# In the routing phase GpSimd, not VectorE, writes the low part of the weight tiles

## The chip, the core and the metric

One core of one Trainium2 chip runs the whole program in one launch. The metric is the device time of that core in microseconds (us); lower is better. TensorE (PE in the profile) multiplies matrices, VectorE (DVE) and ScalarE (ACT) work element by element, GpSimd (POOL) is the fourth compute engine, and SyncE (SP) issues most of the DMAs here.

## What is computed

Two decoder layers over 512 tokens of width 1024, in float32. Each layer has a mixer (a gated MLP and a stick-breaking attention side by side) and then a PEER layer: product keys choose 16 of 16384 single-neuron experts for each of 8 heads of each token. Cut to the PEER layer:

```
q1, q2 = split(h @ w_q)                 # 8 heads, 128 = 64 + 64
s1, s2 = q1 @ k1.T, q2 @ k2.T           # 128 keys each
v1, i1 = top_k(s1, 16); v2, i2 = top_k(s2, 16)
sc, pos = top_k(v1[:, None] + v2[None, :], 16)   # of 256 sums
eidx = i1 * 128 + i2, taken at pos
g = softmax(sc)
y = sum_k g_k * gelu(u_tab[eidx_k] . h) * v_tab[eidx_k]
```

## The kernel before

**How the PEER layer is done.** For 384 of the 512 tokens the kernel gathers no rows: it multiplies all 16384 rows of `u_tab` with the tokens (128 tiles of 128 experts, "ut tiles"), applies GELU, scales by a dense matrix of gates that is zero where an expert was not chosen, and multiplies with all of `v_tab`. The other 128 tokens go by indirect DMAs that GpSimd issues. A layer therefore has three phases: `mixer`, `route_phase` and `dense_phase`.

**Weights in two parts.** TensorE multiplies in a reduced float32 format (`F32R`), so each weight tile of 128x1024 is split into a high part and the rest, and a product takes three matmuls (`mm3`, L308 to L313: hi*hi, lo*hi, hi*lo). The class `Stream` (L51) does this for every weight: `_load` (L61) issues the DMA of a raw tile on SP's queue, `_prep` (L76) lets ScalarE write the high part (`whi`, L83) and VectorE subtract it from the raw tile to get the low part (`wlo`, L84). The pool `wp` has three buffers of each part; `fill` (L92) keeps two tiles prepared ahead of the one that TensorE uses. ScalarE can write a new `whi` once TensorE has done with the tile three places earlier.

**The routing phase** (L623, twice, once for each layer) first computes the queries of the 8 heads (`pq`, 8 weight tiles), their scores against the keys (`sc`), and on VectorE the top 16 of each row of 128 scores (L676 to L680: MAX8, FIND_INDEX8 and MATCH_REPLACE8). Then comes `route` (L715) for each of four blocks of 128 tokens: the top 16 of the candidate sums, and the expert indices by comparisons and sums over `f16` tiles of 128x2048 (L746 to L766). `build` (L793) makes the gate matrix for three blocks: for 24 pieces VectorE writes two one-hot tiles (L806, L807) and scales one by the gates (L809, L810), each 128x2048 `f16`; TensorE multiplies them (`pg`, L816, L817), ScalarE copies the product into `sg` (L818) and a DMA writes it to DRAM. Nothing of this uses GpSimd, but for 32 memsets of constants (L705, L706) after the top 16 of the scores, since their buffers take the place of those that it used.

**What fills TensorE meanwhile.** `prefill` (L635) computes the first 60 ut tiles of the layer (`PRE`, L29) during the routing: 24 matmuls `pA` of 384 columns each, GELU on ScalarE (`ga`, L645), and a DMA to DRAM, from where the dense phase loads them again. `prefill` and the generator `routing` are interleaved by estimated costs (L830 to L841).

**Order.** The program is written in one stream and a scheduler sorts each engine's instructions with a simulated timeline; the instructions of `_prep` get a higher priority (L81). The order on each engine is fixed when the program is built. An engine takes its instructions in that order and waits where one is not ready.

**Dense phase.** The remaining ut tiles and all v tiles go through the same `_prep`; the gates are loaded by `load_g` (L853).

Of the kernel before, what the change touches and what calls it, by code (L numbers as in the profile page):

```python
# [9 lines left out]
F32 = mybir.dt.float32  # L10
# [40 lines left out]
class Stream:  # L51


    def __init__(self, tc, raw, part, entries, dma_ahead, prep_ahead, start=None):
        self.tc, self.nc = tc, tc.nc
        self.raw, self.part = deque(raw), part
        self.src, self.loaded, self.ready, self.plain = deque(entries), deque(), deque(), deque()
        self.da, self.pa = dma_ahead, prep_ahead
        self.start, self.held, self.preps = start, RAW1 if start else 0, 3 if start else 0

    def _load(self):  # L61
        kind, ap = self.src.popleft()
        r = self.raw[0].tile([P, 1024], F32, tag="raw", name="raw")
        self.raw.rotate(-1)
        r = r[:, : ap.shape[-1]]
        if self.held:
            self.held -= 1
            self.start("dma", self.nc.gpsimd.dma_start(r, ap))
        else:
            self.nc.sync.dma_start(r, ap)  # L70
        if kind == "a":
            self.plain.append(r)
        else:
            self.loaded.append((kind, r))

    def _prep(self):  # L76
        kind, r = self.loaded.popleft()
        pool = self.part[kind]
        hi = pool.tile([P, 1024], F32R, tag=f"{kind}hi", name=f"{kind}hi")
        lo = pool.tile([P, 1024], F32R, tag=f"{kind}lo", name=f"{kind}lo")  # L80
        with self.tc.high_priority(offset=HP):  # L81
            n = r.shape[-1]
            i = self.nc.scalar.activation(hi[:, :n], r, AF.Copy)  # L83
            j = self.nc.vector.tensor_sub(lo[:, :n], r, hi.bitcast(F32)[:, :n])  # L84
        if self.preps:
            self.preps -= 1
            late = "" if self.preps else "2"
            self.start("act" + late, i)
            self.start("dve" + late, j)
        self.ready.append((hi, lo))  # L90
# [28 lines left out]
def tile_trunk(ctx, tc, a, dbg=None):  # L119
    nc = tc.nc  # L120
    V, S, G, PE = nc.vector, nc.scalar, nc.gpsimd, nc.tensor
# [31 lines left out]
    def after(i, name):  # L153

        tc.add_manual_dep(i.ins, name, mybir.DependencyInfo(mybir.DependencyClass.NoSync, mybir.DependencyReason.DATA), reason="order")

    def dump(name, t):
        if dbg is not None and name in dbg:
            nc.sync.dma_start(dbg[name], t)
# [448 lines left out]
    def peer(l, ws, part):  # L608
        gd = dram.tile([NK // 4, P, TD // 32, P], F32, name=f"gd{l}")
        sp = dram.tile([PRE, P, TD], F32, name=f"sp{l}")  # L610
        with ExitStack() as outer:
            rk = outer.enter_context(tc.tile_pool(name="rk", bufs=1))
            hs = rk.tile([P, 1024], F32, name="hs")
            eid = rk.tile([P, P], I32, name="eid")
            gs = rk.tile([P, P], F32, name="gs")
            with ExitStack() as st:
                route_phase(l, ws, st, gd, sp, hs, eid, gs)
            with ExitStack() as st:
                dense_phase(l, ws, part, st, gd, sp, hs, eid, gs)
        if l == 0:  # L620
            dump("x2", xT)
# [371 lines left out]
    for l in range(L):  # L993
        part = {"w": wp}
        entries, rest = [], [a["ada_w"][t] for t in SECTIONS[l]]
        tiles = [a["w_all"][l, k] for k in range(28)]
        if l == 0:
            entries = [("a", t) for t in rest[:4]]
            del rest[:4]
            tiles[0:7] = [x for k in range(4) for x in (tiles[k], a["w_u"][k])]  # L1000
        for k, t in enumerate(tiles):
            entries.append(("w", t))
            entries += [("a", t) for t in rest[: ADA_AFTER[l][k]]]
            del rest[: ADA_AFTER[l][k]]
        assert not rest
        for h in range(H):
            entries.append(("w", a["w_all"][l, 28 + h]))
            if h % 2 == 1:
                entries.append(("w", a["ut"][l, h // 2]))
        entries += [("w", a["ut"][l, b]) for b in range(H // 2, PRE)]  # L1010
        for i in range(NK + AHEAD - 1):
            if i < NK and ORDER[i] >= PRE:
                entries.append(("w", a["ut"][l, ORDER[i]]))
            if i >= AHEAD - 1:
                b = ORDER[i - AHEAD + 1]
                entries.append(("v", a[f"v{l}"][b * P : (b + 1) * P, :]))
        ws = Stream(tc, [rawp], part, entries, RAW1 - 1, 2, (lambda k, i: after(i, tails[k])) if l else None)
        mixer(l, ws)
        peer(l, ws, part)
# [59 lines left out]
```

## Time and profile before

| | before |
|---|---|
| median of 3 runs | 2968.13 us (2965.47 to 2970.85) |
| the profiled execution, its own time | 2973.6 us |
| span of its trace | 2971.9 us |
| TensorE (PE) busy, matmuls | 2889.1 us, 97% |
| PE weight loads (PEld) busy | 2496.5 us, 84% |
| VectorE (DVE) busy | 2443.5 us, 82% |
| ScalarE (ACT) busy | 1257.8 us, 42% |
| GpSimd (POOL) busy | 703.9 us, 24% |
| mean granted TensorE clock | 0.988 of full speed |

The time is that of one whole execution; the span runs from the first to the last instruction on the core, 1.7 us less. Busy times are averages over three phases that have different limits. In the trace the routing phase of the first layer lies at about 300 to 676 us, that of the second at about 1770 to 2137 us. Matmuls overlap their successors, so a TensorE that is shown busy is not one that could do no more.

### The profile page before, as it was taken

How to read it: one execution, taken by the hardware profiler on the slowest of the kernel's cores; microseconds unless marked ns; L12 is line 12 of the kernel's file. 1: busy time of each engine (PE TensorE's matmuls, PEld its weight loads, DVE VectorE, ACT ScalarE, POOL GpSimd, SP SyncE). 2: the span in 40 equal slices, each digit the busy share in tenths (PEclk: the TensorE clock that was granted, in tenths of full speed). 3: DMA queues.
4: the chain of work that ended last, by engine and by line, in shares of the span. 5: the costliest groups of instructions: out<-in, count | busy, mean ns of one | idle time of the engine just before them, and what ended most of it. 6: DMA issues, size and time to landing. Idle time of an engine off the chain costs nothing. (4 is left out here: it accounts for less than half of the span.)

```text
span 2971.9 us, 42190 instructions
## 1 busy us (share of the span) xinstructions
PE 2889.1 (97%) x15130; PEld 2496.5 (84%) x15130; DVE 2443.5 (82%) x4584; ACT 1257.8 (42%) x1856; POOL 703.9 (24%) x618
## 2 busy tenths in 40 slices
PE   7998999999999999999999989999999999999998
PEld 5766889998888888888876568999988888888886
DVE  7876899986888888888895659998787878888888
ACT  3564345544333333333245633555533333333332
POOL 1000000002444344344600000000044434443444
PEclk8999999999999999999999999999999999999999
DMA  8832245889999999999874122568999999999995
GB/s 289 286 116 65 68 146 176 261 265 354 355 329 351 332 336 357 331 352 330 291 242 141 43 80 79 172 207 253 287 385 328 354 328 353 340 338 344 334 348 189
DMA packets 317874, 782.62 MB, mean 263 GB/s; under 512 B 24944, under 2 KB 154000, under 8 KB 317664
## 3 DMA queue, kind: packets, MB, share of 16 engines
q1 hardware_dynamic: 125712, 431.02, 41.2%
q0 software_dynamic: 75408, 273.92, 25.0%
q10 hardware_dynamic: 116544, 74.98, 8.4%
q8 instruction: 118, 1.93, 0.3%
q14 instruction: 92, 0.75, 0.1%
HBM read 703.28 MB, written 76.55 MB: 262 GB/s over the span
## 5 line engine op out<-in xcount | busy, mean ns | idle before, releaser
L311 PE MATMUL pA<-hhi,whi 128*128 128x384 f32 x2048 | 692.5, 338 | 12.6 <-ACT ga L645 12.6
L313 PE MATMUL pA<-hhi,wlo 128*128 128x384 f32 x2048 | 693.7, 339 | 4.5 <-DVE wlo L84 4.5
L312 PE MATMUL pA<-hlo,whi 128*128 128x384 f32 x2048 | 691.9, 338 | 0.0
L870 POOL DMA_INDIRECT rows<-in_u,eid x256 | 335.4, 1310 | 1022.3 <-ACT gar L929 560.3
L83 ACT ACTIVATE whi<-raw 128x1024 fp32r<-128x1024 f32 x329 | 346.8, 1056 | 483.1 <-PE pA L312 271.7
L84 DVE TENSOR_TENSOR wlo<-raw,whi 128x1024 fp32r<-128x1024 f32 x329 | 405.3, 1237 | 127.1 <-ACT whi L83 120.2
L952 PE MATMUL yp<-vlo,whi 128*128 128x512 f32 x1536 | 474.3, 390 | 0.0
L952 PE MATMUL yp<-vhi,wlo 128*128 128x512 f32 x1536 | 474.1, 390 | 0.0
L952 PE MATMUL yp<-vhi,whi 128*128 128x512 f32 x1536 | 473.2, 390 | 0.0
L870 POOL DMA_INDIRECT rows<-in_v,eid x256 | 339.6, 1327 | 437.2 <-DVE junk L879 366.6
L311 PEld LDWEIGHTS pA<-hhi,whi 128*128 128x128 f32 x2048 | 386.7, 189 | 19.2 <-ACT ga L645 13.6
L313 PEld LDWEIGHTS pA<-hhi,wlo 128*128 128x128 f32 x2048 | 386.0, 189 | 7.4 <-DVE wlo L84 6.8
L312 PEld LDWEIGHTS pA<-hlo,whi 128*128 128x128 f32 x2048 | 386.4, 189 | 5.7
L941 ACT ACTIVATE whi<-gar 128x384 fp32r<-128x384 f32 x256 | 133.7, 523 | 540.8 <-PE yp L952 394.4
L84 DVE TENSOR_TENSOR vlo<-raw,vhi 128x1024 fp32r<-128x1024 f32 x256 | 312.6, 1223 | 48.9 <-ACT vhi L83 39.6
L952 PEld LDWEIGHTS yp<-vlo,whi 128*128 128x128 f32 x1536 | 288.3, 188 | 62.2
L952 PEld LDWEIGHTS yp<-vhi,wlo 128*128 128x128 f32 x1536 | 288.2, 188 | 61.4
L952 PEld LDWEIGHTS yp<-vhi,whi 128*128 128x128 f32 x1536 | 286.5, 188 | 51.4
L886 DVE SCALAR_TENSOR_TENSOR ys<-rows,wsp,ys 128x1024 f32<-128x1024 f32 x254 | 325.2, 1280 | 0.9
L879 DVE SCALAR_TENSOR_TENSOR junk<-rows,hs 128x1024 bf16<-128x1024 f32 x256 | 312.2, 1219 | 10.0 <-DMA rows<-in_u,eid 9.7
L83 ACT ACTIVATE vhi<-raw 128x1024 fp32r<-128x1024 f32 x256 | 270.8, 1059 | 82.8 <-PE yp L952 78.9
L942 DVE TENSOR_TENSOR wlo<-gar,whi 128x384 fp32r<-128x384 f32 x256 | 142.4, 557 | 98.3 <-ACT whi L941 91.0
(243 smaller groups left out, 3783.2 us busy)
## 6 DMA issues: line engine op xcount, KB each, us to landing
raw<-in_ut SPq DMA_DIRECT2D x256, 512.0 KB
raw<-in_v SPq DMA_DIRECT2D x256, 512.0 KB
gd<-sg ACTq DMA_DIRECT2D x24, 2048.0 KB
gt<-gd SPq DMA_DIRECT2D x64, 768.0 KB
raw<-in_ada_w SPq DMA_DIRECT2D x94, 512.0 KB
raw<-in_w_all SPq DMA_DIRECT2D x66, 512.0 KB
sp<-ga ACTq DMA_DIRECT2D x120, 192.0 KB
gar<-sp SPq DMA_DIRECT2D x120, 192.0 KB
```

The source lines that it names most:

```text
L83: i = self.nc.scalar.activation(hi[:, :n], r, AF.Copy)
L84: j = self.nc.vector.tensor_sub(lo[:, :n], r, hi.bitcast(F32)[:, :n])
L311: PE.matmul(ps, w[0][:, sl], hhi[:, m, :n], start=first, stop=False)
L312: PE.matmul(ps, w[0][:, sl], hlo[:, m, :n], start=False, stop=False)
L313: PE.matmul(ps, w[1][:, sl], hhi[:, m, :n], start=False, stop=last)
L870: tails["dma"] = G.indirect_dma_start(out=r, out_offset=None, in_=table, in_offset=bass.IndirectOffsetOnAxis(ap=eid[:, k : k + 1], axis=0) ...
L879: tc.keep_in_program_order(V.scalar_tensor_tensor(junk, r, 1.0, hs, ALU.mult, ALU.mult, accum_out=dots[:, k : k + 1]))
L886: tc.keep_in_program_order(V.scalar_tensor_tensor(ys, r, wsp[:, k : k + 1], ys, ALU.mult, ALU.add))
L941: S.activation(whi, ga, AF.Copy)
L942: V.tensor_sub(wlo, ga, whi.bitcast(F32))
L952: PE.matmul(yp[tb][e], w[wq][:, tt], vt[vq][:, e * T : (e + 1) * T], start=(i == 0 and wq + vq == 0), stop=(i == NK - 1 and wq == 1))
```

## The change

`Stream` gets a field `rest`, the engine that writes the low part, VectorE by default. Around `route_phase` it is set to GpSimd, so all weight tiles prepared there (68 in each layer: 6 of the 8 query tiles, the 60 ut tiles, and the first 2 of the dense phase) have their low part written by GpSimd. The operation, its operands and its buffers stay the same. From L60 on the lines of the changed kernel stand one lower, from L618 on three.

```diff
@@ -57,6 +57,7 @@
         self.da, self.pa = dma_ahead, prep_ahead
         self.start, self.held, self.preps = start, RAW1 if start else 0, 3 if start else 0
+        self.rest = tc.nc.vector
@@ -81,7 +82,7 @@
             i = self.nc.scalar.activation(hi[:, :n], r, AF.Copy)
-            j = self.nc.vector.tensor_sub(lo[:, :n], r, hi.bitcast(F32)[:, :n])
+            j = self.rest.tensor_sub(lo[:, :n], r, hi.bitcast(F32)[:, :n])
@@ -614,7 +615,9 @@
             with ExitStack() as st:
+                ws.rest = G
                 route_phase(l, ws, st, gd, sp, hs, eid, gs)
+                ws.rest = V
             with ExitStack() as st:
                 dense_phase(l, ws, part, st, gd, sp, hs, eid, gs)
```

The scheduler sorts the program anew. **GpSimd's queue**, first layer, before: after the mixer's mask (L339) it holds the key tables (`kb`) and the memsets.

```order
L339 AFFINE_SELECT wT<-wT 128x1024
L629 MEMSET kb 128x256
L630 DMA kb<-in_k1T 64x128
L631 DMA kb<-in_k2T 64x128
L705 MEMSET stE 128x128
L706 MEMSET ioJ 128x128
```

Now, with the low parts in it:

```order
L632 MEMSET kb 128x256
L633 DMA kb<-in_k1T 64x128
L634 DMA kb<-in_k2T 64x128
L85 TENSOR_TENSOR wlo<-raw,whi 128x1024 x15
L708 MEMSET stE 128x128
L709 MEMSET ioJ 128x128
...
L85 TENSOR_TENSOR wlo<-raw,whi 128x1024 x53
L873 DMA rows<-in_u,eid 128x1024 x33
```

Fifteen low parts (6 query tiles, ut tiles 1 to 9) stand ahead of the 32 memsets and 53 behind them; ahead of the gathers of the dense phase nothing else is new.

**VectorE's queue** at the first piece of `build` in the first layer (`o` are the one-hot tiles, `gh` and `gl` the scaled ones), before:

```order
L84 TENSOR_TENSOR wlo<-raw,whi 128x1024
L712 TENSOR_TENSOR ex_3805<-ex_3805 128x512
L806 TENSOR_TENSOR o_3959<-ioT,it 128x2048
L807 TENSOR_TENSOR o_3960<-ioT,it 128x2048
L806 TENSOR_TENSOR o_4044<-ioT,it 128x2048
L712 TENSOR_TENSOR ge<-ge 128x1024
L740 TENSOR_TENSOR ex<-sc_4707 128x128
L712 TENSOR_TENSOR ex_3805<-ex_3805 128x256
L84 TENSOR_TENSOR wlo<-raw,whi 128x1024
L809 TENSOR_TENSOR gh<-o_3960,it 128x2048
L810 TENSOR_TENSOR gl<-o_3960,it 128x2048
```

Now:

```order
L809 TENSOR_TENSOR o_3959<-ioT,it 128x2048
L810 TENSOR_TENSOR o_3960<-ioT,it 128x2048
L715 TENSOR_TENSOR ex_3805<-ex_3805 128x512
L809 TENSOR_TENSOR o_4044<-ioT,it 128x2048
L715 TENSOR_TENSOR ge<-ge 128x1024
L785 SCALAR_TENSOR_TENSOR pk<-ex,pk 128x128
L812 TENSOR_TENSOR gh<-o_3960,it 128x2048
L813 TENSOR_TENSOR gl<-o_3960,it 128x2048
```

The low parts are gone and the rest keeps its order but for small swaps.

**TensorE's queue** where the gate matrix begins in the first layer (`pg`), before:

```order
L311 MATMUL pA<-hhi,whi 128x384
L312 MATMUL pA<-hlo,whi 128x384
L816 LDWEIGHTS gh
L816 MATMUL pg<-o_3959,gh 128x128
L816 LDWEIGHTS gh
L816 MATMUL pg<-o_3959,gh 128x128
```

Now:

```order
L314 MATMUL pA<-hhi,wlo 128x384
L312 MATMUL pA<-hhi,whi 128x384
L819 LDWEIGHTS gh
L819 MATMUL pg<-o_3959,gh 128x128
L819 LDWEIGHTS gh
L819 MATMUL pg<-o_3959,gh 128x128
```

The rows look alike; what moved is their place. Counted from the phase's start, 31.5 ut tiles of 24 `pA` matmuls stood ahead of the first `pg` before and 23.0 now. The last `pg` stood behind all 60 tiles before; now it stands behind 54.6, so 5.4 tiles come after it.

## Rows read from the trace of the kernel before

**Rows 1.** The page, busy time and share of each engine.
```profile
PE 2889.1 (97%) x15130; PEld 2496.5 (84%) x15130; DVE 2443.5 (82%) x4584; ACT 1257.8 (42%) x1856; POOL 703.9 (24%) x618
```

**Rows 2.** Busy time by stretch, first layer: us, then busy (instructions) by engine, clock, DMA.
```profile
317.00:408.00 91.00, 84.51 (x423) 76.18 (x422) 89.96 (x527) 30.01 (x46) 0.20 (x1) 0.96 0.32 102
408.00:492.00 84.00, 84.00 (x488) 83.69 (x487) 82.95 (x388) 47.86 (x57) 4.74 (x32) 1.00 0.53 170
492.00:675.00 183.00, 178.00 (x1515) 168.93 (x1513) 161.66 (x167) 101.58 (x165) 0.00 (x0) 1.00 0.82 250
```

**Rows 3.** The same stretches, VectorE's instructions of line 84 alone (low parts).
```profile
317.00:408.00 91.00, 17.54 (x13) 0.96 0.32 102
408.00:492.00 84.00, 24.73 (x20) 1.00 0.53 170
492.00:675.00 183.00, 38.00 (x31) 1.00 0.82 250
```

**Rows 4.** Busy time by stretch, finer, columns PE, PEld, DVE, ACT, POOL, clock.
```profile
375.00:390.00 15.00, 11.53 (x64) 10.76 (x62) 15.00 (x92) 3.96 (x6) 0.00 (x0) 1.00 0.32 98
390.00:405.00 15.00, 11.99 (x55) 11.48 (x56) 15.00 (x74) 4.80 (x7) 0.00 (x0) 0.77 0.47 146
420.00:435.00 15.00, 15.00 (x88) 15.00 (x87) 15.00 (x68) 8.54 (x11) 0.00 (x0) 1.00 0.50 165
...
1845.00:1860.00 15.00, 8.95 (x43) 8.13 (x42) 15.00 (x92) 3.67 (x6) 0.00 (x0) 0.84 0.31 96
```

**Rows 5.** Who waited for whom, 255 to 690 us: us, times, longest.
```profile
ACT ss L672 <- DVE ti L680: 24.0, 6, 7.1
...
PE pA L311 <- ACT ga L645: 6.4, 2, 5.6
...
PE pg L816 <- ACT sg L818: 4.6, 4, 1.4
```

**Rows 6.** GpSimd and VectorE in order of time around the mask, first and second layer.
```profile
15.03 1.87 POOL L339 TENSOR_SCALAR_AFFINE_SELECT wT<-wT 128x1024 f32<-128x1024 f32 x1 [3.81 <-DMA wT<-in_sgu_w]
...
15.87 1.57 DVE L289 TENSOR_TENSOR sq<-sq 128x512 f32<-128x512 f32 x1
...
1497.10 2.16 POOL L339 TENSOR_SCALAR_AFFINE_SELECT wT<-wT 128x1024 f32<-128x1024 f32 x1 [3.98 <-DMA wT<-in_sgu_w]
...
1495.95 2.36 DVE L84 TENSOR_TENSOR wlo<-raw,whi 128x1024 fp32r<-128x1024 f32 x2 [1.70 <-ACT whi L83]
```

**Rows 7.** Line 289 in the whole span: count, ns min/median/max.
```profile
L289 DVE TENSOR_TENSOR sq<-sq x9: 684/687/1569, 6.5 to 1742.1; 128x512 f32<-128x512 f32 x9
```

**Rows 8.** GpSimd's first of 32 memsets in `route`, and a VectorE copy beside them.
```profile
407.80 0.30 POOL L705 MEMSET stE<- 128x128 f16 x1 [142.02 <-PE pA L313]
...
408.51 3.21 DVE L721 COPY d<-i 128x8 f16<-128x8 f16 x1
```

**Rows 9.** VectorE's groups with one tensor input, 408 to 492 us: busy us, mean ns.
```profile
L734 DVE FIND_INDEX8 pos<-sc,cand 128x8 uint32<-128x50 f32 x32 | 6.1, 226 | 0.0
...
L736 DVE MAX8 sc<-cand 128x8 f32<-128x50 f32 x32 | 4.2, 228 | 0.0
```

**Rows 10.** VectorE's groups, 492 to 676 us, with idle time before them and its releaser.
```profile
L84 DVE TENSOR_TENSOR wlo<-raw,whi 128x1024 fp32r<-128x1024 f32 x32 | 39.2, 1226 | 9.0 <-ACT whi L83 9.0
...
L809 DVE TENSOR_TENSOR gh<-o,it 128x2048 f16<-128x2048 f16 x24 | 29.4, 1223 | 7.8 <-PE pg L816 7.8
...
L752 DVE TENSOR_TENSOR ex<-ge,ex 128x2048 f16<-128x2048 f16 x1 | 1.2, 1225 | 5.0 <-ACT ex L751 5.0
```

**Rows 11.** The instructions of `pg`, 400 to 700 us: first and last start.
```profile
L816 PE MATMUL pg<-o,gh x384: 217/218/236, 501.5 to 674.9; 128*128 128x128 f16 x192
```

**Rows 12.** Line 645 from 285 to 407.6 us: the first eight GELUs of ut tiles.
```profile
L645 ACT ACTIVATE ga<-pA x8: 470/475/490, 317.0 to 404.5; 128x384 f32<-128x384 f32 x8
```

## Prediction

> **What bounds the kernel now.** The page comes first: TensorE is busy 97% of the span, VectorE 82%, GpSimd 24% [rows 1]. So TensorE bounds the kernel, and work moved between other engines pays only where TensorE waits for them. The view by stretch shows where that could be. I cut the first layer's routing into the top 16 of the scores (317 to 408 us), the first passes of `route` (408 to 492) and the builds (492 to 675). VectorE is busy 90.0 of 91 us, 83.0 of 84 and 161.7 of 183 [rows 2]. TensorE loses 6.5 us in the first stretch, nothing in the second and 5.0 in the third [rows 2]. The finer view puts the first loss at 375 to 405 us: 3.5 and 3.0 us idle, and then a granted clock of 0.77 (in a slice with both its levels, 1.2 and 2.4 GHz), which costs 0.23 * 15 = 3.4 us [rows 4]. The view of waits names the cause: ScalarE's copies of the scores (`ss`) wait for VectorE's top 16, and behind them in ScalarE's queue stands the GELU `ga` that TensorE needs to get a PSUM buffer back, 6.4 us [rows 5]. So the first layer holds some 10 us that a faster VectorE can give back; in the second layer the same place is idle for 6.0 us of a slice and the clock falls to 0.84, some 8.5 us [rows 4]. The third stretch's loss is mostly `pg` waiting for ScalarE, 4.6 us [rows 5]; I leave it. All that can be won is about 19 us.
>
> **What it removes.** VectorE's low parts in the three stretches: 17.5, 24.7 and 38.0 us, 64 instructions [rows 3]. What is left to VectorE is 90.0 - 17.5 = 72.4 us, 83.0 - 24.7 = 58.2 and 161.7 - 38.0 = 123.7 [rows 2, 3]. The top 16 then ends at 317 + 72.4 = 389, not 408, and TensorE's 10 us there come back. Without any conflict VectorE would be through with the rest at 389 + 181.9 = 571, far ahead of TensorE.
>
> **What it adds.** The same subtractions on GpSimd, which has nothing else to do there. Two costs need a price.
>
> First, one low part there. The trace has no GpSimd instruction with two inputs; the nearest of that size is the mask of 128x1024 float32, one input: 1.87 and 2.16 us as recorded [rows 6]. Part of that is waiting (next paragraph). Without it the first ran from about 15.9 to 16.90 and the second from the end of VectorE's two low parts, 1495.95 + 2.36 = 1498.31, to 1499.26: about 1.0 us. The lower end is 1.0 us, if a second input is free; the upper end 2 * 2.16 = 4.3, if no part of the record is waiting and each input costs all of it. I take 2 * 1.0 and 0.2 for start and handover (short memsets of 128 columns take 0.30 with it [rows 8]): 2.2 us, since both records fit a net 1.0. The Trainium skill (GPSIMD Engine Reference, Elementwise — side-by-side cycle accounting) gives 4497 ns for a `tensor_tensor` of 2048 float32; half of it, 2.25 us, is my estimate from that page, and the time by it would be some 4 us longer than forecast.
>
> Second, what it does to VectorE meanwhile. Line 289, an addition with two SBUF inputs of 128x512, takes 684 to 687 ns in the median and 1569 once [rows 7]. That once is at 15.87, with the mask running on GpSimd from 15.03 to 16.90 [rows 6]: it ends at 17.44, 0.54 us after the mask. The mask in turn ends 0.95 us after the second low part in the second layer [rows 6]. So a GpSimd instruction that reads SBUF and a VectorE instruction with two SBUF inputs go one after the other. A VectorE copy of 8 columns took 3.21 us beside the memsets too [rows 8]. The Trainium skill states this as a rule (SBUF — State Buffer, Who interferes with whom): the two share one port pair, whoever starts first holds it for the whole instruction, and a VectorE instruction with two SBUF inputs contends with a GpSimd instruction that reads SBUF. Line 289's 1569 ns agrees; by this rule the sum is the one below, and without it the first rival's time comes out.
>
> **The sum, first layer.** From 389 on VectorE has 181.9 us of its own work. Instructions with one input run beside GpSimd: three groups of FIND and REPLACE of about 6.0 us and two of MAX8 of about 4.2, 26 us [rows 9]. GpSimd has 48 low parts in that time: the order puts 15 ahead of the memsets; the last `pg` stands behind 54.6 ut tiles, with three buffers GpSimd is then at tile 57, its 63rd, and 63 - 15 = 48. They hold the port for 48 * 2.2 = 106 us. An ut tile takes TensorE 24 matmuls at 88 per 15 us [rows 4], 4.1 us, so GpSimd is at work 54% of the time and 0.54 * 26 = 14 us of the 106 fall beside one-input work: VectorE is held up by 92. Add the waits for TensorE and ScalarE that VectorE has in the builds anyway, 7.8 + 5.0 us (its 9.0 on `whi` go) [rows 10]: 389 + 182 + 92 + 13 = 676, and 1 or 2 for the last `pg`. It was at 675 before [rows 11]. But now 5.4 ut tiles stand behind it in TensorE's fixed order, 5.4 * 4.1 = 22 us, of which before none did. So the phase ends at some 700 and not 676: **+24 us**. TensorE by itself would have its last `pg` at 675 - 10 - 4.6 - 22 = 638, so it waits for VectorE some 38 us, about half of it before the first `pg`: TensorE comes there at 501.5 - 8.5 * 4.1 - 10 = 457 [rows 11], VectorE with its 58 + 4 us and 17 low parts between (37 us, 14 beside one-input work) at 474.
>
> A new wait in GpSimd's queue: its 16th low part (ut tile 10) stands behind the 32 memsets, which wait for the top 16 to end and take 0.2 + 4.7 us [rows 2]. 389 + 5 + 2.2 = 396; TensorE wants it when 9 ut tiles are done, which was at 404.5 - 10 + 4.1 = 399 [rows 12]. So nothing, or up to 4 us if the top 16 ends later. ScalarE does what it did, SP's queue loads the same tiles, and GpSimd's gathers come after the phase.
>
> The second layer runs the same code with almost the same order: again +24. The profiled execution took 2973.6 us, 5.5 above the median; 2973.6 + 48 = 3022, and on the median **3016 us**.
>
> **The rivals.** *No conflict, or a cheap one* (0.20): the two engines run side by side, or a low part takes GpSimd at most 1.3 us. VectorE's chain then ends before TensorE's 638, TensorE never waits, and the losses at the top 16 come back: 2968 - 10 - 8.5 = 2949. For it speaks that the conflict is seen in one instruction of VectorE and two of GpSimd only, and with another operation; against it that those three fit to a tenth of a microsecond. *It balances* (0.08): the hold-up per layer is 41.7 times the price (48 less the 14 us' share); at 92 the phase is 24 us late, so it breaks even at 68 us, a price of 1.63. Between 1.3 and 1.6 the time is 2949 to 2968. *The top 16 conflicts too* (0.09): MAX8, FIND and REPLACE would have to wait for GpSimd as well; no row here shows them beside a reading GpSimd instruction. Then 15 low parts delay the first stretch by 33 us a layer: 3016 + 66 = 3082. The Trainium skill's section named above has such one-input instructions free of the conflict; by that rule this rival falls away, and no run here shows it. *The upper price* (0.05): at 4.3 us GpSimd is slower than TensorE's 4.1 per tile and all is serial, 389 + 156 + 206 + 13 + 22 = 786, so 110 us a layer: 3188. That the change does not do what it says is no case: the built queues show the low parts on GpSimd.
>
> **How the numbers follow.** My forecast (0.58) covers prices of 1.7 to 2.8 us, +3 to +49 a layer: 2974 to 3066, likeliest 3016. Slower by over 0.2% (6 us, about what a measurement of this kernel can tell): 0.57 of it and the last two rivals, 0.71. Within 0.2%: 0.01 of the forecast and most of the balance, 0.07. Faster: the rest of the balance and no conflict, 0.22. The range runs from the first rival with a few us for the other small waits, 2946, to the third, 3080; outside lie the upper price, and half of the cases near the ends. The slower cases alone span 2974 to 3066.
>
> **What the profile will show.** If right: `wlo` on GpSimd at 2 to 3.5 us as recorded; VectorE's 128x2048 instructions with a mean well over 1.23 us in the builds, and those of MAX8 unchanged; the top 16 ending near 389; TensorE waiting for `gh` for tens of us, the longest wait at the first `pg`; the last `pg` near 676 and no `pg` beside the last five ut tiles. If VectorE's 128x2048 mean stays at 1.23, the conflict is not there and I am wrong; if TensorE waits for `wlo`, GpSimd is the bound.

## The result and the profile after

The changed kernel takes 3056.12 us in the median of four runs (3053.45 to 3062.77), the kernel before 2968.93 in the same comparison: a ratio of 1.0292, 95% interval 1.0276 to 1.0307, **87 us slower**. The profiled execution has a span of 3054.3 us. From the page (busy times, then the group of the low parts on GpSimd) and from the list of `wlo`'s instructions (ns min/median/max):

```profile
PE 2916.0 (95%) x15130; PEld 2519.7 (82%) x15130; DVE 2463.3 (81%) x4448; ACT 1259.3 (41%) x1856; POOL 1079.5 (35%) x754
...
L85 POOL TENSOR_TENSOR wlo<-raw,whi 128x1024 fp32r<-128x1024 f32 x136 | 373.4, 2751 | 502.6 <-ACT whi L84 480.8
...
L85 POOL TENSOR_TENSOR wlo<-raw,whi x136: 2340/2491/6715, 288.3 to 2215.2; 128x1024 fp32r<-128x1024 f32 x136
```

136 low parts went to GpSimd (the page of before had it at 24% [rows 1]), and yet VectorE is *busier* than before, 2463 us against 2443, with 136 instructions less. The shortest low part takes 2.34 us on GpSimd; I take this as its time when nothing holds it up.

The same cut by stretch as before [rows 2], first layer, with the borders where the events now lie: top 16, `route` up to the first `pg`, builds, and a new last stretch behind the last `pg`. Columns are us, then busy (instructions) of PE, PEld, DVE, ACT, POOL, then clock.

```profile
317.00:392.00 75.00, 75.00 (x384) 67.81 (x384) 74.31 (x509) 28.26 (x43) 29.03 (x13) 1.00 0.34 111
392.00:488.00 96.00, 74.18 (x374) 71.56 (x373) 93.44 (x379) 41.18 (x46) 49.14 (x48) 0.87 0.38 121
488.00:691.00 203.00, 188.88 (x1537) 178.85 (x1538) 183.27 (x131) 103.43 (x167) 94.65 (x32) 0.96 0.73 226
691.00:714.00 23.00, 22.17 (x128) 21.85 (x127) 0.00 (x0) 8.31 (x12) 12.15 (x6) 1.00 0.94 310
```

The first stretch is 16 us shorter and TensorE loses nothing in it any more, as intended. Then TensorE is idle for 21.8 us of 96 and 14.1 of 203, and its mean granted clock falls to 0.87 and 0.96. In the finer view the clock (between the levels of 2.4 and 1.2 GHz) falls with the slices in which TensorE waited; before, the slice 420 to 435 stood at 1.00 [rows 4]:

```profile
420.00:435.00 15.00, 8.08 (x31) 7.35 (x30) 14.73 (x78) 9.09 (x10) 7.00 (x3) 0.66 0.28 89
...
450.00:465.00 15.00, 10.74 (x44) 10.45 (x44) 14.86 (x50) 5.63 (x7) 7.89 (x3) 0.70 0.40 141
```

Who made TensorE wait from 300 to 720 us (us, times, longest), to be held against [rows 5]:

```profile
PE pA L312 <- ACT ga L648: 10.1, 3, 6.9
PE pg L819 <- DVE o L809: 7.3, 3, 4.5
PE pg L819 <- DVE gh L812: 5.7, 1, 5.7
PE pg L819 <- ACT sg L821: 5.2, 4, 2.3
PE pt L790 <- DVE pk L716: 4.7, 3, 4.3
PE pA L314 <- POOL wlo L85: 3.3, 2, 1.8
```

VectorE's products (`o`, `gh`, `pk`) are new here, 18 us; GpSimd itself is hardly waited for. The longest single wait, 6.9 us for `ga`, leads back to VectorE as well. ScalarE's queue stands for 10.83 us at the broadcast `ex` until VectorE has summed `pk`, the GELU that TensorE needs comes behind it in that queue, and TensorE goes on with it at 429.08:

```profile
422.75 1.91 ACT L766 ACTIVATE ex<-i 128x2048 f16<-128x2048 f16 x1 [10.83 <-DVE pk L716]
...
428.54 0.49 ACT L648 ACTIVATE ga<-pA 128x384 f32<-128x384 f32 x1
...
429.08 0.69 PE L312 MATMUL pA<-hhi,whi 128*128 128x384 f32 x1 [6.92 <-ACT ga L648]
```

Why VectorE is late is seen in order of time: VectorE first, then GpSimd, in the same stretch (start, duration).

```profile
564.49 1.21 DVE L812 TENSOR_TENSOR gh<-o,it 128x2048 f16<-128x2048 f16 x1
565.62 1.21 DVE L813 TENSOR_TENSOR gl<-o,it 128x2048 f16<-128x2048 f16 x1
566.75 2.42 DVE L716 TENSOR_TENSOR pk<-ex 128x128 f16<-128x128 f16 x1
569.10 3.42 DVE L810 TENSOR_TENSOR o<-ioT,it 128x2048 f16<-128x2048 f16 x1
...
565.80 5.64 POOL L85 TENSOR_TENSOR wlo<-raw,whi 128x1024 fp32r<-128x1024 f32 x2 [4.00 <-ACT whi L84]
```

GpSimd's first low part is recorded from 565.80 on, while `gl` runs. If it starts its work only when `gl` ends at 566.83, two times 2.34 behind that give 571.5, and its row ends there (565.80 + 5.64). VectorE's `pk`, an addition of 128 columns, stands for 2.42 us until the first low part is through, and `o` for 3.42, that is 2.2 behind the second low part and its own 1.2. Here the two engines take turns, one whole instruction at a time. The four 128x2048 groups of `build` on VectorE have means of 1.49 to 1.86 us from 300 to 760 us (before 1.22 for `gh` [rows 10]), and its additions of 128x1024 (line 715) 2.27, in e3 below 0.68:

```profile
L809 DVE TENSOR_TENSOR o<-ioT,it 128x2048 f16<-128x2048 f16 x24 | 44.5, 1856 | 0.1
L812 DVE TENSOR_TENSOR gh<-o,it 128x2048 f16<-128x2048 f16 x24 | 41.7, 1737 | 10.8 <-PE pg L819 9.5
L810 DVE TENSOR_TENSOR o<-ioT,it 128x2048 f16<-128x2048 f16 x24 | 39.7, 1655 | 0.5
...
L715 DVE TENSOR_TENSOR ex<-ex 128x1024 f16<-128x1024 f16 x8 | 18.1, 2267 | 0.0
```

The top 16, which has one tensor input, is left alone (317 to 392 us): its MAX8 has 297 ns in the median and 326 at most beside 13 low parts on GpSimd, no more than in the kernel before (second row, 317 to 408 us).

```profile
L682 DVE MAX8 tv<-ss x64: 281/297/326, 322.4 to 391.2; 128x8 f32<-128x128 f32 x64
...
L679 DVE MAX8 tv<-ss x64: 275/404/569, 322.7 to 406.3; 128x8 f32<-128x128 f32 x64
```

Where the first layer's phase ends, by VectorE's last product `gl`, the matmuls of `pg` (before 501.5 to 674.9 [rows 11]) and the GELUs of the ut tiles, after and then before (first and last start):

```profile
681.57 1.21 DVE L813 TENSOR_TENSOR gl<-o,it 128x2048 f16<-128x2048 f16 x1
```

```profile
L819 PE MATMUL pg<-o,gh x384: 218/218/330, 488.4 to 690.3; 128*128 128x128 f16 x192
```

```profile
L648 ACT ACTIVATE ga<-pA x60: 466/473/516, 316.7 to 714.1; 128x384 f32<-128x384 f32 x60
...
L645 ACT ACTIVATE ga<-pA x60: 467/472/522, 317.0 to 675.5; 128x384 f32<-128x384 f32 x60
```

In the kernel before, the last GELU came at 675.5, so the first layer loses 38.6 us. The second loses 41.3 more: its first and last GELU stand at 1821.8 and 2219.2, before at 1781.0 and 2137.1. Together this is 80 of the 82 us between the spans of the two traces.

### The profile page after: what moved, and what is told of

It is laid out like the page before. It is cut to its first block, busy times and chain, and to the rows that moved or that the text cites. A ratio compares the mean times of both kernels' runs of the same rounds, so it can differ in the third digit from the quotient of the medians.

```text
span 3054.3 us, 42232 instructions
## 1 busy us (share of the span) xinstructions
PE 2916.0 (95%) x15130; PEld 2519.7 (82%) x15130; DVE 2463.3 (81%) x4448; ACT 1259.3 (41%) x1856; POOL 1079.5 (35%) x754
## 5 line engine op out<-in xcount | busy, mean ns | idle before, releaser
L312 PE MATMUL pA<-hhi,whi 128*128 128x384 f32 x2048 | 702.4, 343 | 20.4 <-ACT ga L648 20.4
L314 PE MATMUL pA<-hhi,wlo 128*128 128x384 f32 x2048 | 702.9, 343 | 6.9 <-POOL wlo L85 6.9
L85 POOL TENSOR_TENSOR wlo<-raw,whi 128x1024 fp32r<-128x1024 f32 x136 | 373.4, 2751 | 502.6 <-ACT whi L84 480.8
L314 PEld LDWEIGHTS pA<-hhi,wlo 128*128 128x128 f32 x2048 | 392.2, 192 | 9.9 <-POOL wlo L85 9.3
L313 PEld LDWEIGHTS pA<-hlo,whi 128*128 128x128 f32 x2048 | 392.7, 192 | 5.9
L85 DVE TENSOR_TENSOR wlo<-raw,whi 128x1024 fp32r<-128x1024 f32 x193 | 235.4, 1222 | 160.7 <-ACT whi L84 155.4
```

Source lines behind the costliest of these rows:

```text
L85: j = self.rest.tensor_sub(lo[:, :n], r, hi.bitcast(F32)[:, :n])
L312: PE.matmul(ps, w[0][:, sl], hhi[:, m, :n], start=first, stop=False)
L313: PE.matmul(ps, w[0][:, sl], hlo[:, m, :n], start=False, stop=False)
L314: PE.matmul(ps, w[1][:, sl], hhi[:, m, :n], start=False, stop=last)
```

## The experiments

The theory is the one of the prediction: GpSimd's reading of SBUF and VectorE's instructions with two SBUF inputs hold each other up. The rivals: GpSimd's being late, the changed order of the queues, or ScalarE's queue. All medians are held against a kernel before of 2970 to 2971 us in the same comparison.

**The two halves of the change alone.** e1 has GpSimd write the low parts during the top 16 only:

```diff
+            ws.rest = V
             with ExitStack() as s2:
```

> GpSimd writes the low parts only while the top 16 of the scores is found; from the first passes of route on VectorE writes them again. Theory (GpSimd's reads and VectorE's instructions with two SBUF inputs hold each other up, MAX8, FIND and REPLACE not): the top 16 ends 15 us earlier as in the changed kernel, TensorE's 10 + 8.5 us there come back, nothing is held up later: 2949 us, 2943 to 2958, last pg near 665. Rival (a low part on GpSimd is late for TensorE whatever VectorE does, or the queues' new order costs the time): part of the 87 us stays, 2975 or more.

Measured: **2957.9 us, ratio 0.996 (0.9947 to 0.9974), faster than both kernels**. TensorE's waits from 300 to 720 us are down to this, and no stretch has a clock below 1.00:

```profile
PE pA L312 <- ACT ga L648: 2.9, 1, 2.9
PE pg L820 <- ACT sg L822: 2.3, 5, 0.9
PE pA L314 <- DVE wlo L85: 1.1, 2, 1.0
```

Of the 18.5 us that the rows of before promised, 12.7 came. GpSimd's low part does no harm beside the top 16. e2 is the other half: VectorE writes the low parts during the top 16, GpSimd from there on.

```diff
+            ws.rest = G
             with ExitStack() as s2:
...
-                ws.rest = G
                 route_phase(l, ws, st, gd, sp, hs, eid, gs)
```

> The other part alone: VectorE writes the low parts during the top 16, GpSimd from there on. Theory: the top 16 ends at 407 again and the 13 or so low parts of that stretch no longer help, while the hold-up behind it stays, so the first pg and the last pg come some 10 to 18 us a layer later than in the changed kernel: 3075 to 3090. Rival (the top 16 itself suffers from GpSimd's low parts): this version is faster than the changed kernel, under 3050.

Measured: 3071.4 us, 1.0339 (1.0318 to 1.0361), 101 us slower; a little below the expected range, with its two runs 10 us apart: what GpSimd brings during the top 16 is worth some 15 us to the change, not 19 or more. The halves add up: -12.7 + 100.8 = 88, and the change has 87.

**Does reading hold VectorE up?** e3 keeps GpSimd about as busy and the order of the queues the same, but reads nothing:

```diff
-            j = self.rest.tensor_sub(lo[:, :n], r, hi.bitcast(F32)[:, :n])
+            if self.rest is self.nc.vector:
+                j = self.rest.tensor_sub(lo[:, :n], r, hi.bitcast(F32)[:, :n])
+            else:
+                j = self.rest.memset(lo[:, :n].bitcast(F32), 0.0)
+                j = self.rest.memset(lo[:, :n].bitcast(F32), 0.0)
```

> Leaves out the subtraction in the two routing phases: in its place GpSimd writes the low part with two memsets of 128x1024 (some 2 us together, an estimate from the 128x128 memset's 0.15), so that it writes as long but reads no SBUF; the order of every queue stays that of the changed kernel. Theory (it is GpSimd's reading that holds VectorE up): VectorE's 128x2048 instructions go back to a mean near 1.23, last pg under 650, 2945 to 2960. Rival 1 (any GpSimd work there holds VectorE up): 3030 to 3060. Rival 2 (writes hold up only VectorE's copies and casts): a few us over 2950, with the copies of route at 2 us and more.

Measured: 2997.6 us, 1.0091 (1.0073 to 1.0109). The mechanism is as the theory has it: the second of VectorE's 128x2048 comparisons `o`, with a mean of 1655 ns in the change (line 810), is back to a median of 1224 ns and 1228 at most, though GpSimd writes 1.9 us for each tile. So it is GpSimd's *reads* that hold up VectorE's two-input instructions. But the time is not the expected 2945 to 2960: 27 us over the kernel before are left, with TensorE waiting for ScalarE. First VectorE's group, then TensorE's waits (300 to 720 us):

```profile
L814 DVE TENSOR_TENSOR o<-ioT,it x48: 1167/1224/1228, 458.9 to 2114.6; 128x2048 f16<-128x2048 f16 x48
```

```profile
PE pg L823 <- ACT sg L825: 9.1, 4, 4.0
PE pA L316 <- ACT ga L652: 8.6, 4, 3.0
```

e4 replaces the subtraction by one copy, so one input and not two:

```diff
-            j = self.rest.tensor_sub(lo[:, :n], r, hi.bitcast(F32)[:, :n])
+            j = self.rest.tensor_copy(lo[:, :n], r)
```

> Leaves out the subtraction in the two routing phases: in its place GpSimd writes the low part as one copy of the raw tile, one SBUF input and not two, order of the queues unchanged. By the mask's record it should take GpSimd about 1.0 us. Theory (the hold-up is GpSimd's time at the port, 41.7 times the price a layer, and 68 us break even): 42 us, so TensorE bounds again, 2945 to 2962. Rival (each hand-over costs VectorE a fixed time, whatever the length): over 3000.

Measured: 2998.0 us, 1.0092 (1.0074 to 1.0111). The copy takes 1.03 us on GpSimd at least, less than half of the subtraction with its two inputs. VectorE's four groups of `build` have means of 1.25 to 1.46 us, between e3's and the change's, and the time is e3's to half a microsecond. So a price of 1 us is indeed below the break-even: from 390 to 720 us VectorE waits 58.7 us for TensorE at `gh` in e3 and 47.2 in e4, so it is not the bound of the builds in either.

```profile
DVE gh L816 <- PE pg L823: 58.7, 15, 18.6
...
DVE gh L815 <- PE pg L822: 47.2, 15, 17.8
```

That both stand on one floor of 2998 is read from the two times alone. The expectation was wrong about where that floor lies.

**How much for how many.** e12 lets GpSimd write only every second low part behind the top 16 (`_prep` swaps the two engines after each tile there):

```diff
+            if self.alt is not None:
+                self.alt, self.rest = self.rest, self.alt
             j = self.rest.tensor_sub(lo[:, :n], r, hi.bitcast(F32)[:, :n])
```

> As in the changed kernel during the top 16; from then on GpSimd writes every second low part only and VectorE the others. Theory (the hold-up is proportional to GpSimd's time at the port): behind the top 16 24 low parts of 1.22 on VectorE and 24 of 2.34 on GpSimd, with 3 beside one-input work: 392 + 182 + 29 + 53 + 16 = 672 for the last pg against 690, 18 us a layer less: 3020, 3005 to 3030. Rival (a few of GpSimd's reads in the wrong place set the end, whatever their number): 3045 or more.

Measured: 3019.5 us, 1.0165 (1.0146 to 1.0184), with the last `pg` at 670.4 (expected 672). This fits a hold-up that grows with GpSimd's time at the port, and not the rival. The expectation took the prediction's sum with the start and the price that the change's trace had shown; it met this variant's time to a microsecond and its last `pg` to two.

```profile
L822 PE MATMUL pg<-o,gh x384: 217/218/331, 484.2 to 670.4; 128*128 128x128 f16 x192
```

**The order and the tail.** e5 spreads the routing's work over all ut tiles, so that none stands behind the last `pg`:

```diff
-                TOTAL = (4 * 22.0 + 24 * 4.4) / 0.93
+                TOTAL = (4 * 22.0 + 24 * 4.4) / 1.03
```

> The changed kernel with the routing's work spread over all of TensorE's tiles (TOTAL divided by 1.03 in place of 0.93), so that no ut tile stands behind the last pg instead of 5.4; the first pg stays behind 23 tiles. Theory (VectorE's chain with the hold-up sets the last pg, the tail comes on top): the tail of 23.7 us goes, but 5.4 more low parts hold VectorE up ahead of the last pg, 5.4 * 2.34 * 0.87 = 11 us, so some 12 us a layer come back: 3032, 3022 to 3044. Rival (the tail is TensorE work that must be done anyway and TensorE bounds): no change, 3050 to 3062.

Measured: 3035.2 us, 1.022 (1.0177 to 1.0263): some 10 us a layer come back by the medians, close to the 12 expected, and 8 from first to last GELU in the traces. The last `pg` comes 11 us later, behind 5.4 more low parts, and nothing follows it:

```profile
L819 PE MATMUL pg<-o,gh x384: 218/218/312, 483.7 to 701.2; 128*128 128x128 f16 x192
```

e7 gives TensorE the order of the kernel before in full, e8 does the same to e3:

```diff
-                TOTAL = (4 * 22.0 + 24 * 4.4) / 0.93
+                TOTAL = (4 * 22.0 + 24 * 4.4) / 1.03
...
-                        want = TOTAL * (prefilled[0] - 1 - first + (q + 1) / 8) / (PRE - first)
+                        want = TOTAL * ((prefilled[0] - 1 - first + (q + 1) / 8) / (PRE - first)) ** 1.5
```

> The changed kernel with the routing's work paced so that TensorE's order is that of the kernel before: the first pg behind 31.4 tiles (before 31.5, changed 23.0), the middle one behind 48.9 (48.1, 40.3), the last behind 60 (60, 54.6). GpSimd still writes every low part. Theory (hold-up): VectorE's chain stays the bound, 392 + 182 of its own work + 53 low parts * 2.34 less 14 + 13 of waits = 697 for the last pg and no tail, 17 us a layer less than now: 3022, 3012 to 3045. Rival (the order is the whole cause, VectorE's hold-up fits beside TensorE): under 2985.

> Leaves out the subtraction in the two routing phases (two memsets on GpSimd in its place, as in e3) and has TensorE's order of the kernel before, as in e7. With e3 (2998), the changed kernel and e7 it makes a square of order by hold-up. Theory (what e3 lost is the order: pg stands too early in TensorE's queue for VectorE and ScalarE): the 27 us over before go and the 10 + 8.5 us at the top 16 come back, 2952, 2945 to 2962. Rival (GpSimd's writing or its waits in the queue cost the 27 us): 2985 or more.

Measured: e7 3047.2 us, 1.0261 (1.0219 to 1.0302); e8 2982.8 us, 1.0042 (1.0027 to 1.0058). e7 misses its range, and the last `pg` comes at 708.3 and not 697. With `pg` so late in TensorE's order VectorE itself waits: it stands still for 26 us of the 313.5 from the end of the top 16 to its last `gl` (388.5 to 702.0), 16.6 of them for `pg`, where the sum had 13 for all its waits.

```profile
DVE gh L812 <- PE pg L819: 13.8, 1, 13.8
...
DVE o L809 <- PE pg L820: 2.8, 1, 2.8
```

e8 lies between its two expectations. Together they make a square:

| us | GpSimd subtracts | two memsets |
|---|---|---|
| TensorE's order of the change | 3056.1 | 2997.6 |
| TensorE's order of before | 3047.2 | 2982.8 |

By the table the hold-up costs 58 and 64 us, TensorE's order 9 and 15. The 9 is not clear of the spread: e7's interval and the change's (1.0276 to 1.0307) overlap. From first to last GELU, both layers added, the four traces take 795, 739, 792 and 722 us, so there the order is worth 3 us under the subtraction and 17 with the memsets. What is left, 2982.8 - 2970.2 = 13 us (and the gain at the top 16 that does not show), is neither; in the traces it is 722 against 715 us in these stretches.

**ScalarE's queue.** Two attempts on the waits for `ga`. e6 gives `ex1` and `ex2` two buffers:

```diff
-                    ex1 = tmp.tile([P, 16, P], F16, tag="ex1", name="ex1")
+                    ex1 = tmp.tile([P, 16, P], F16, tag="ex1", name="ex1", bufs=2)
```

> The changed kernel with two buffers for ex1 and ex2 in place of one, so that ScalarE's broadcasts need not wait until VectorE has summed the last one. Theory for the 14 us a layer that the forecast missed ahead of the first pg (ScalarE's queue stands at ex until VectorE is through, and whi, ga and so GpSimd's low parts wait behind it): ScalarE's waits for pk, 31 us in the first layer, go, and 5 to 14 us a layer come back: 3028 to 3046. Rival (VectorE is busy 93.4 of 96 us there, and what ScalarE waits for is not what sets the end): no change, 3050 to 3062.

Measured: 3055.7 us, 1.0289 (1.0248 to 1.033): no change. ScalarE's waits for `pk` in the first layer were 35 us, against 31 in the change, so the edit did not take away what it was meant to take, and it leaves the queue's part open; that VectorE is the bound there fits. e15 takes the broadcasts off ScalarE in e3:

```diff
-                    S.activation(k4(ex1), bc(d1), AF.Copy)
-                    V.tensor_tensor(ex1, ge, ex1, op=ALU.mult)
+                    V.tensor_tensor(k4(ex1), k4(ge), bc(d1), op=ALU.mult)
```

> As e3 (two memsets on GpSimd, the subtraction left out in the two routing phases), and ScalarE's broadcasts ex1 and ex2 left away: VectorE multiplies with the broadcast operand directly, the same result. e3 and e8 were slower than the kernel before though VectorE's 128x2048 instructions were not held up, with TensorE waiting for ga 8 to 9 us and for sg 8 to 9 us in the first layer. Theory (ScalarE's queue stands at ex until VectorE has the operand, and ga and whi wait behind it; without VectorE's low parts ex is set earlier there): TensorE's waits for ga go, 5 to 10 us a layer: 2980, 2970 to 2988. Rival (it is TensorE's order or the buffers that cost the 27 us): 2992 or more.

Measured: 2984.1 us, 1.0042 (1.0027 to 1.0056), 13 us less than e3, as the theory has it. TensorE's order hardly moved (the first `pg` stands behind 23.9 ut tiles, in e3 behind 23.1). In the first layer TensorE's wait for `ga` is halved; the one for `sg` stays. From first to last GELU the two layers are 7 us shorter than in e3, of 11 between the spans, so not all of the gain is shown to come from there.

```profile
PE pg L821 <- ACT sg L823: 9.4, 5, 4.1
PE pA L316 <- ACT ga L652: 4.3, 2, 3.0
```

**For a faster kernel.** e16 is e1 with the edit of e15, e9 is e1 with the pacing of e7.

> As e1 (GpSimd writes the low parts during the top 16 only, which took 2957.9), and ScalarE's broadcasts ex1 and ex2 left away as in e15; computes the whole reference. Theory (ScalarE's waits at ex cost TensorE what is left there, ga 2.9 and clock): 2950, 2944 to 2957. Rival (VectorE's two multiplications a block become dearer with a broadcast operand, and VectorE is busy 95 of 96 us there): 2960 to 2985.

> As e1 (GpSimd writes the low parts during the top 16 only, 2957.9), with the routing's work paced as in e7: the first pg behind 30.1 tiles (e1 29.6), the middle one behind 49.0 (46.3), the last behind 60 (58.0). e1 brought 12.7 us where the rows of before promised 18.5; what is left in its first layer is TensorE waiting for ga 2.9, sg 2.3 and wlo 1.1. Theory (pg and its copies sg are still too dense at the end of e1's order): 2954, 2948 to 2959. Rival (what is left are ScalarE's turns between whi, ga and sg in any order): 2956 to 2968.

Measured: e16 2967.7 us (0.999, 0.9981 to 0.9999), e9 2966.2 us (0.9987, 0.9978 to 0.9996). Both lose most of e1's gain. In e16 VectorE's multiplication with a broadcast operand takes 2.29 us against 1.22, and TensorE's wait for `sg` grows from 2.3 to 7.5 us. e1 stays the best version.

```profile
L766 DVE TENSOR_TENSOR ex<-ge,i 128x2048 f16<-128x2048 f16 x4 | 9.1, 2286 | 0.0
```

## Why the prediction was right, and where its sum was off

**Right: the sign and the mechanism.** The forecast was 3016 us, 48 over the kernel before; measured are 87, inside the range of 2974 to 3066 but near its upper end. VectorE and GpSimd take turns as the mask's rows let expect [rows 6, 7]; the top 16 is not touched; TensorE waits for VectorE and not for GpSimd; the tail behind the last `pg` is there, 714.1 - 690.4 = 23.7 us where 22 were worked out. The Trainium skill (SBUF — State Buffer, Who interferes with whom) names both halves, a VectorE instruction with two SBUF inputs contends with a GpSimd instruction that reads and not with one that only writes. The change and e3 agree: a mean of 1655 ns (line 810) against a median of 1224 (line 814) for the same instruction.

TensorE was to wait for `gh` for tens of us, the longest time at the first `pg`. It stands idle for 36.9 us from first to last GELU of the first layer, but `gh` is waited for only 5.7 of them, at the first `pg`, and 10.1 go by way of `ga`.

**The price.** 2.2 us forecast, 2.34 measured, 6% more. It was put together as two inputs of 1.0 us; e4's copy, with one input, takes 1.03, so that step was right too. The Trainium skill (GPSIMD Engine Reference, Elementwise — side-by-side cycle accounting) has 4497 ns for twice the columns; half of it, 2.25 us as an estimate, is 4% low.

**VectorE's sum.** Behind the top 16 VectorE is busy 93.4 + 183.3 = 276.7 us; less its own 181.9 the hold-up is 94.8, forecast 92. It started 3 us later than forecast (392 and not 389) and waited about 14, forecast 13. It ended its last `gl` at 682.8; the sum had 676. So this chain was off by 7 us a layer.

**The step that was mis-sized: +24 us a layer, measured +38.6 and +41.3.** Of the 15 us that are missing in the first layer, 7 are VectorE's, as above. 6 more are the last `pg`: the forecast let it follow VectorE by 1 or 2 us, but it came 7.6 us behind. The last 2 us are the tail. From 675 to 691 us TensorE was busy without a gap, so it had a backlog of its own:

```profile
675.00:691.00 16.00, 16.00 (x140) 15.21 (x140) 7.64 (x5) 8.93 (x15) 7.68 (x3) 1.00 0.83 263
```

TensorE's own account names the term. From first to last GELU, first and second layer, before and then after (us, busy of PE first):

```profile
317.00:675.50 358.50, 346.66 (x2422) 328.79 (x2420) 334.56 (x1080) 179.94 (x266) 4.95 (x32) 0.99 0.63 194
1781.00:2137.10 356.10, 347.04 (x2424) 328.58 (x2422) 335.09 (x1080) 180.46 (x267) 4.95 (x32) 0.99 0.63 195
...
316.70:714.10 397.40, 360.53 (x2422) 340.37 (x2420) 351.02 (x1016) 181.59 (x268) 185.27 (x98) 0.95 0.59 184
1821.80:2219.20 397.40, 360.21 (x2424) 339.91 (x2422) 349.92 (x1016) 181.38 (x268) 185.30 (x98) 0.95 0.59 185
```

In the first layer TensorE is idle for 25.0 us more than before, in the second for 28.1. The forecast had that about right: 38 us of new waits, less the 6.5 and 4.6 that it gave back, are 27. But the same number of matmuls also takes 13.9 and 13.2 us longer. This is the granted clock: weighted with TensorE's busy time in the stretches above, it costs 0.13 * 74.2 + 0.04 * 188.9 = 17.2 us in the first layer, before 0.04 * 84.5 = 3.4 [rows 2]. The forecast gave back those 3.4 us [rows 4] and charged nothing for a clock that falls in the new waits. So the term that it put at nothing is 17 us; with 2 us less of idle time than forecast, that is the difference between +24 and what was measured. That the slower matmuls make the backlog which delays the last `pg` is read from the rows; no run shows it by itself, and at a full clock part of that time would have been waiting, since VectorE was through only at 682.8.

**The rivals.** *No conflict, or a cheap one* falls by the timeline; but its time was wrong too. It was put at 2949, and e3 and e4, where VectorE is no longer the bound, take 2998. With VectorE's low parts gone, the scheduler set `pg` earlier (the first behind 23.0 ut tiles and not 31.5, as e7's expectation says), and TensorE waits for `ga` and `sg` from ScalarE. I priced this rival by VectorE's chain alone and did not ask what the new order does to ScalarE. As far as e3 and e4 can stand for a change without the conflict, it would still have been some 1% slower. *The top 16 conflicts too* falls by MAX8's 297 ns. *The upper price* of 4.3 falls by 2.34. *The balance* could not be seen: at 1.0 us (e4) the floor of the order already lies above the kernel before.

**GpSimd's queue.** The wait of the 16th low part behind the 32 memsets was put at 0 to 4 us; TensorE waits for `wlo` 3.3 us in all.

**Open:** what the last 13 us of e8 and e15 are. Both still show TensorE waiting for `sg` 8 to 9 us in the first layer, against 4.6 before [rows 5]. In e3, e4, e8 and e15 the low part does not wait for `whi` either, so their queues move earlier in a way that no subtraction could.

## What to carry to other kernels

In this kernel, moving an element-wise operation with two inputs from VectorE to GpSimd relieved VectorE only while it ran instructions with one SBUF input; behind the top 16 each 2.34 us on GpSimd cost VectorE some 2.0, more than the 1.23 that the operation took on VectorE. Move it for the stretch where the other engine does one-input work, and only there: that was worth 0.4% here, where the whole move cost 2.9%. And a scheduler that knows nothing of the conflict orders the other queues for a VectorE that it believes free, so price the new order too, and the clock that TensorE can lose with its waits.

## What had not been expected of the hardware

GpSimd's memsets read nothing and in e3 leave VectorE's 128x2048 instructions alone, but a VectorE copy or cast can stand still beside them, and for longer than one of them. In e3 a cast of 128 columns on VectorE (a like one takes 0.26 us at 420.49, with no memset ahead of it) starts at 392.64 and ends at 398.02; in that time 11 memsets, short ones and then 5 of 0.95 us, follow each other without a gap until 397.94. A copy of 8 columns stands for 3.23 us just ahead of it. VectorE first, then GpSimd:

```profile
389.37 3.23 DVE L728 COPY d<-i 128x8 f16<-128x8 f16 x1
...
392.64 5.38 DVE L725 CAST i<-ti 128x128 f16<-128x128 uint32 x1
...
393.43 1.83 POOL L88 MEMSET wlo<- 128x1024 f32 x2
395.21 1.83 POOL L89 MEMSET wlo<- 128x1024 f32 x2
397.00 0.94 POOL L88 MEMSET wlo<- 128x1024 f32 x1
```

The Trainium skill (SBUF — State Buffer, Who interferes with whom) has the port held for the whole instruction. Here VectorE's copy and its cast each got through only after many memsets in a row, so the measurement goes further than the rule. The copy of 3.21 us beside the short memsets in the kernel before [rows 8] looks the same.
